# Three branch projections as Strassen pairs, summed by accumulating stores, in a hybrid decoder layer

## The chip, the cores and the metric

One core of one Trainium2 chip runs the whole program. The metric is the device time of one execution in microseconds (us). The kernel before took 1414.16, 1417.39 and 1422.7 us in three runs, median 1417.39.

## The reference

One layer of a decoder for 1024 prompt rows and 8 sample rows, all in float32. Three branches (gated linear attention "GLA", pooling, cross-attention) each give rows of width 1024; each is projected, multiplied by its own gate, and the three are added:

```python
proj = h @ w_in
...
branches = jnp.stack([br_gla, br_pool, br_x], axis=2)
bproj = jnp.einsum('btnw,nwd->btnd', branches, w_branch)
gates = jax.nn.sigmoid(merge.astype(jnp.float32)).reshape(B, T, N_BRANCH, D_MODEL)
merged = jnp.sum(gates * bproj.astype(jnp.float32), axis=2).astype(x.dtype)
y = merged @ w_out
return x + y, S.astype(x.dtype), new_hist
```

A last RMSNorm over x + y ends the program. The branch rows of GLA carry a per-channel gain (`gla_gain`).

## The kernel before, in words

**Numbers.** Every float32 operand of a large product is split into a high and a low part (`split`, L223 on ACT for the high part, L224 on DVE for the low one), and a product is three matmuls (`mm3`, L242 to L244): high by high, high by low, low by high.

**Pairs.** All the wide products up to the merge are done in pairs (`Pair`): a pair makes 256 output columns for all 1032 rows, by seven products of a Strassen-Winograd scheme. One product is 2 column halves by 4 steps by 3 matmuls, each 128 x 258. `seq` lists the products: (i, 1) to (i, 4), then (i+1, 0), then (i, 5) and (i, 6). `run_product` saves partial sums from PSUM with ACT (r1, r2, r3 at L686) and adds them up with DVE (L768, L787, L792, L797, L808 in the cases j = 1, 4, 5, 6). Product 1 to 4 end in the tile c1, which is finished in product 4; products 5 and 6 end in c2, finished in product 6. Products 0, 2 and 4 share the accumulator p.x, products 3 and 5 the accumulator p.z: product 5 adds to p.z, which the sums of product 4 have read together with r3.

Pairs 0 to 39 multiply by w_in and store their results to DRAM scratch: queries, keys, merge gates (`m_scr`), gated branch rows (`br_scr`). Pairs 40 to 43 project the cross-attention branch, pairs 44 to 47 the pooling branch (`ORDER` = 2, 1, 0). In `finish` the results are multiplied by sigmoid(merge), loaded by `factors` as tiles sg (L823) and passed through ACT (`sigmoids`); the product on DVE is L717, and the store to `acc_scr` is a DMA issued by POOL (L728), one for c1 and one for c2 of each pair. Between two branches `turnover` loads the next branch's rows and splits them as right-hand operands (tiles b and x by SP, v11, v21, v22 and four differences), spread over the products of the pairs around it.

**Units.** The third branch, GLA, is done in eight plain units of 128 output columns: eight steps over the inner dimension, three matmuls, chunks of 384, 384 and 264 rows. `branch_k` loads and splits the operand during the last pairs, with the gain applied in the split (L226, L227); `fetch` loads weights (wbr), gates (sig) and the two earlier sums (acc, acm) for a unit ahead; DVE adds and multiplies (L1598, L1606, L1607). The merged rows stay in SBUF and are split there (`mg_split`, tiles mg0h, mg0l and on), with a small copy on POOL of the sample columns (mgs).

**Output.** Sixteen blocks of 24 matmuls, 512 wide, multiply by w_out (column half hf 0, then hf 1), started for two row blocks in an inner range of 5 and then the rest (`begun`). The sample rows are two short blocks (8 and 9, L1662) that multiply by unsplit weights (wos, L1629). SP loads w_out (wor), the wos tiles, the final gain fg and the rows of x that are added (y, L1671). Each block is added to y by DVE (L1686) and squared by ACT (L1687); the norm follows and the stores.

**What sets the order.** PE and SP run in program order. ACT, DVE and POOL are ordered by a scheduler, held by `issue_after` edges. Buffers: pool E has 30 of 128 x 1032, ring R 15 of 128 x 516; PSUM accumulators PX six.

Of the kernel before, what the change touches and what calls it, by code (L numbers as in the profile page):

```python
# [40 lines left out]
O_Q, O_K, O_V, O_G, O_A, O_U, O_PG, O_XQ, O_XG, O_M = (  # L41
    0, 512, 1024, 2048, 3072, 3088, 4112, 5136, 6160, 7184)
EW = 1032
NBR = 2
EXP_LN_SET = 6


# [1 line left out]
def trunk_kernel(ctx: ExitStack, tc: tile.TileContext,  # L49
# [151 lines left out]
    PAIR = (P, 4, HT)  # L201
    xq_scr, v_scr = scratch(NH, "xqs", (NS, 256)), scratch(NH, "vs", (NS, 256))
    pt_scr = scratch(4 * NH, "pts", (8, 32, 4, 64))
    acc_scr = [scratch(4, f"acc{n}_", PAIR) for n in range(2)]
    mkv_scr = [scratch(NH, f"mkvs{o}", (P, 2, DV)) for o in range(2)]
    al_scr = scratch(2, "als", (P, HT))
    alp_scr = scratch(2, "alps", (P, 512))
# [124 lines left out]
        pairs += [Pair(cols_of(off + 2 * P * j), br_scr[n][j], gated=(n, j)) for j in range(4)]  # L332
    pairs.append(pairs.pop(27))
    for o, n in enumerate(ORDER[:NBR]):
        pairs += [Pair(w_branch[n][:, 2 * P * j:2 * P * (j + 1)], acc_scr[o][j], branch=(o, n, j)) for j in range(4)]
    NPAIR = len(pairs)
    TURNS = {39 + 4 * o: ORDER[o] for o in range(NBR)}

# [340 lines left out]
    def run_product(n):  # L679
# [18 lines left out]
        def finish(t, e):  # L698
            rows = (slice(0, 4, 3), slice(1, 3))[e]
            if p.s0 is not None:  # L700
                nc.gpsimd.tensor_copy(diagonal(smp[:, NS * p.s0:], e), t[:, :, 512:HT])
            if p.gated:
                n, g = p.gated
                for i in range(2):
                    ch, hf = divmod((0, 3, 1, 2)[2 * e + i], 2)
                    m = p.mix[e][i]
                    if n == 0:
                        x = m.rearrange("p (q w k) -> p w q k", q=4, w=4)
                        y = t[:, i, :512].rearrange("p (w q k) -> p w q k", q=4, w=4)
                        nc.vector.tensor_tensor(y, y, x, op=ALU.mult)  # L710
                    else:
                        nc.vector.tensor_tensor(t[:, i, :512], t[:, i, :512], m, op=ALU.mult)
                ss = diagonal(brs[n].rearrange("p k b -> p (k b)")[:, 2 * NS * g:], e)
                nc.vector.tensor_tensor(t[:, :, 512:HT], t[:, :, 512:HT], ss, op=ALU.mult)
            if p.branch:
                for i, sg in enumerate(p.mix[e]):
                    nc.vector.tensor_tensor(t[:, i], t[:, i], sg, op=ALU.mult)  # L717
            if p.turned:
                for i in range(2):
                    ch, hf = divmod((0, 3, 1, 2)[2 * e + i], 2)  # L720
                    r = R([512], name="vt")
                    nc.vector.transpose(r, t[:, i, :512])
                    for q in range(4):
                        c0 = ch * P + 32 * q
                        nc.gpsimd.dma_start(out=p.dst[512 * hf:512 * hf + 512, c0:c0 + 32].rearrange("(t r) c -> r t c", r=32),
                                            in_=r[32 * q:32 * q + 32].rearrange("r (t c) -> r t c", c=32))
                return
            nc.gpsimd.dma_start(out=p.dst[:, rows, :], in_=t)  # L728
# [791 lines left out]
    def branch_k(n, k):  # L1520
        hi, lo = E([2, HT], F32R, name=f"bh{n}"), E([2, HT], F32R, name=f"bl{n}")
        for hf in range(2):
            row = br_scr[n][k // 2][:, 2 * (k % 2) + hf]
            raw = loaded(row[:, :512], [512], "brr")
            split(hi[:, hf, :512], lo[:, hf, :512], raw, None if n else ggain[:, k:k + 1])
        nc.sync.dma_start(out=brs[n][:, k].rearrange("p (h b) -> p h b", h=2),
                          in_=br_scr[n][k // 2][:, 2 * (k % 2):2 * (k % 2) + 2, 512:HT])
        split(hi[:, :, 512:HT], lo[:, :, 512:HT], brs[n][:, k].rearrange("p (h b) -> p h b", h=2))
        return hi.rearrange("p h t -> p (h t)"), lo.rearrange("p h t -> p (h t)")

    units = [(o, ORDER[o], d) for o in range(NBR, 3) for d in range(NK)]
    inputs = {}

    def fetch(u):
        o, n, d = units[u]
        raw = RAW("wbr").rearrange("p a b -> p (a b)").rearrange("p (k n) -> p k n", k=NK)
        nc.sync.dma_start(out=raw, in_=w_branch[n][:, d * P:(d + 1) * P].rearrange("(k p) n -> p k n", p=P))
        w = []
        for i in range(2):
            h, l = W2("wbh"), W2("wbl")  # L1540
            split(h, l, raw[:, 4 * i:4 * i + 4])
            w.append((h, l))
        sig = E([TT], name="sig")
        nc.sync.dma_start(out=sig.rearrange("p (h t) -> p h t", h=2), in_=m_scr[n][d // 2][:, 2 * (d % 2):2 * (d % 2) + 2])
        acc = E([TT], name="acc")
        nc.sync.dma_start(out=acc.rearrange("p (h t) -> p h t", h=2),
                          in_=acc_scr[o - 1][d // 2][:, 2 * (d % 2):2 * (d % 2) + 2])
        more = [loaded(acc_scr[0][d // 2][:, 2 * (d % 2) + q], [HT], "acm") for q in range(2)] if NBR == 2 else []
        inputs[u] = w, sig, acc, more


    br = []
    for n in range(5, len(seq)):
        for _ in range({7: 2, 5: 1, 4: 1, 3: 1, 2: 1, 1: 1}.get(len(seq) - n, 0)):
            br.append(branch_k(ORDER[NBR], len(br)))
        if n == len(seq) - 2:
            fetch(0)
        emit(n)
        turnover(*seq[n])
    br.append(branch_k(ORDER[NBR], 7))  # L1560

    mg, late = [None] * NK, []
    mgs = R([NK, 32], name="mgs")
    for k in range(0, NK, 4):
        nc.gpsimd.memset(mgs[:, k:k + 4], 0.0)

    def mg_split(d, s):
        hi, lo = E([TT], F32R, name=f"mg{d}h"), E([TT], F32R, name=f"mg{d}l")
        split(hi, lo, s)
        mg[d] = hi, lo  # L1570
        nc.gpsimd.tensor_copy(mgs[:, d, :NS].rearrange("p (h b) -> p h b", h=2),
                              s.rearrange("p (h t) -> p h t", h=2)[:, :, 512:HT])

    wo = {}

    def w_out_unit(k, hf):
        raw = loaded(w_out[k * P:(k + 1) * P, 512 * hf:512 * hf + 512], [512], "wor", WS)
        if hf and k < 4:
            hi, lo = (W2("wo").rearrange("p a b -> p (a b)") for _ in range(2))
        elif hf:  # L1580
            e = E([2, 512], F32R, name="woe")
            hi, lo = e[:, 0], e[:, 1]
        elif k < 2:
            hi, lo = V([512], F32R, "woh"), V([512], F32R, "wol")
# [5 lines left out]
    for u, (o, n, d) in enumerate(units):  # L1590
        if d == 0 and o > NBR:
            br = [branch_k(n, k) for k in range(NK)]
        if u + 1 < len(units):
            fetch(u + 1)
        w, sig, acc, more = inputs.pop(u)
        act(sig, sig, AF.Sigmoid)
        for q, x in enumerate(more):
            nc.vector.tensor_tensor(acc[:, q * HT:(q + 1) * HT], acc[:, q * HT:(q + 1) * HT], x, op=ALU.add)  # L1598
        ts = [PX() for _ in CH]
        for k in range(NK):  # L1600
            lh, ll = (x[:, k % 4, :] for x in w[k // 4])
            for t, (c0, cw) in zip(ts, CH):
                mm3(t[:, :cw], lh, ll, br[k][0][:, c0:c0 + cw], br[k][1][:, c0:c0 + cw], k == 0, k == NK - 1)
        for t, (c0, cw) in zip(ts, CH):
            cs = slice(c0, c0 + cw)
            nc.vector.tensor_tensor(sig[:, cs], t[:, :cw], sig[:, cs], op=ALU.mult)  # L1606
            nc.vector.tensor_tensor(sig[:, cs], acc[:, cs], sig[:, cs], op=ALU.add)  # L1607
        if o < 2:
            nc.gpsimd.dma_start(out=acc_scr[o][d // 2][:, 2 * (d % 2):2 * (d % 2) + 2],
                                in_=sig.rearrange("p (h t) -> p h t", h=2))  # L1610
        else:
            if d < 5:
                mg_split(d, sig)
            else:
                late.append((d, sig))
            if d >= 2:
                w_out_unit(d - 2, 0)
    w_out_unit(6, 0)
    w_out_unit(7, 0)
    for d, s in late:  # L1620
        mg_split(d, s)
    own = []

    def own_weights(i):
# [5 lines left out]
            own.extend([w[:, 0], w[:, 1]])  # L1630

    own_weights(0)
    for k in range(NK):
        w_out_unit(k, 1)


    exp_ln_table()
# [9 lines left out]
            mm3(t[:, :b - a], th, tl, wh, wl, k == 0, k == NK - 1)  # L1647


    begun = [PX() for _ in range(2)]  # L1650
    for ks in (range(5), range(5, NK)):
        for tb in range(2):
            row_block(begun[tb], tb, 0, 0, 512, ks)
    for hf, order in enumerate(ORDERS):
        for tb in order:
            m = P if tb < 8 else NS
            if tb >= 8:
# [1 line left out]
                if tb == 8:  # L1659
                    ts = PX()  # L1660
                for j in range(4):
                    nc.tensor.matmul(ts[32 * j:32 * j + 32], lhsT=mgs[:, 4 * (tb - 8) + j], rhs=own.pop(0),  # L1662
                                     start=tb == 8, stop=tb == 9)
                if 2 * hf + tb < 11:
                    own_weights(2 * hf + tb - 7)
# [14 lines left out]
            for b in ends:  # L1680
                t = ts if tb == 8 else begun.pop(0) if begun else PX()
                cs = slice(512 * hf + a, 512 * hf + b)
                if tb < 8 and (hf or tb > 1):
# [58 lines left out]
```

## Time and profile before

| | |
|---|---|
| median of three runs | 1417.39 us (1414.16 to 1422.7) |
| profiled execution | 1417.57 us, span 1415.9 us, mean granted TensorE clock 0.992 |
| pairs 40 to 47 | 1064.46 to 1223.96 us |
| the eight units | 1223.96 to 1314.31 us |
| output, norm, last stores | 1314.31 to 1415.9 us |

The page gives for each engine its busy time, the span in 40 slices with the granted clock, the DMA queues, the chain of work that ended last, the costliest groups of instructions and the DMA issues with their median time to landing. A window view gives the busy time of each engine in a stretch. A row of the timeline is start, duration, engine, line, operation, output<-inputs, and in brackets the idle time before it and what ended it. DMA landing times are min, median and max over the transfers of a view. PE is the tensor engine's matmul side, PEld its weight loads, SPq and POOLq the queues of SyncE and GpSimd.

### The profile page before, as it was taken

Reading aid. Unit: us, or ns where it says so; the run is one execution under the profiler, and the core shown is the slowest. Engines: PE = TensorE matmul, PEld = TensorE weight load, DVE = VectorE, ACT = ScalarE, POOL = GpSimd, SP = SyncE. Lnnn points to the kernel's source line nnn. Section 1 sums busy time; section 2 is a strip of 40 time slices with the busy share of each in tenths; the row PEclk is TensorE's granted clock in tenths of the full one; section 3 lists DMA queues with packets and bytes.
Section 4 is the critical chain, followed back from the end, with each engine's and each line's share of the span. In section 5 each row is a group of like instructions: output and inputs, shape, how many; then the busy total and the mean of one; then the engine's idle time right before and its main releaser. Section 6 shows DMA issues by size and latency. Waiting matters only on the chain.

```text
span 1415.9 us, 29040 instructions
## 1 busy us (share of the span) xinstructions
PE 1390.2 (98%) x10817; PEld 1330.9 (94%) x10817; DVE 997.1 (70%) x2216; ACT 717.9 (51%) x1680; POOL 298.9 (21%) x529
## 2 busy tenths in 40 slices
PE   7999999999999999999999999999999999999998
PEld 6899898999899999999999999999999999999776
DVE  6966675758587777776766769786698896765336
ACT  6744444444466666655654544444456474632222
POOL 4254221335442232222231110101000000000000
PEclk9999999999999999999999999999999999999999
DMA  9367776967656455555555555468557785863633
GB/s 337 125 209 233 241 233 215 282 212 219 179 157 193 142 163 174 156 177 153 165 162 160 171 175 180 160 196 253 174 187 267 222 285 182 289 206 119 225 118 114
DMA packets 188377, 276.45 MB, mean 195 GB/s; under 512 B 20476, under 2 KB 132116, under 8 KB 188228
## 3 DMA queue, kind: packets, MB, share of 16 engines
q1 hardware_dynamic: 115420, 149.31, 33.9%
q0 software_dynamic: 26208, 78.94, 15.8%
q10 hardware_dynamic: 46608, 46.34, 11.4%
q8 instruction: 85, 1.39, 0.4%
q14 instruction: 56, 0.46, 0.1%
HBM read 192.18 MB, written 82.80 MB: 194 GB/s over the span
## 4 chain that ended last, share of the span: by engine, by line
PE 88%; DMA 6%; DVE 3%; issue 1%; ACT 1%; POOL 0%; SPq 0%; DVEq 0%; ACTq 0%
PE px L242 25%; PE px L243 25%; PE px L244 25%; PE pz L243 2%; PE pz L244 2%; PE pz L242 2%; DMA raw<-in_w_in_dram 2%; PE pz L1135 1%; PE pz L1114 1%; DMA wm<-in_w_mv_dram 1%; DMA qb<-xqs 1%; PE pz L962 1%; PE pz L1116 1%; DMA x<-brsc 1%; PE pz L467 0%
## 5 line engine op out<-in xcount | busy, mean ns | idle before, releaser
L686 ACT ACTIVATE r<-px 128x258 f32<-128x258 f32 x288 | 107.7, 377 | 62.4 <-PE px L244 58.1
L242 PE MATMUL px<-ot,s1h 128*128 128x258 f32 x320 | 94.0, 294 | 0.0
L303 DVE TENSOR_TENSOR ws<-raw 128x512 f32<-128x512 f32 x96 | 65.8, 686 | 39.1 <-DMA raw<-in_w_in_dram 27.7
L242 PE MATMUL px<-o,s4h 128*128 128x258 f32 x320 | 92.8, 290 | 0.0
L242 PE MATMUL px<-o,a11h 128*128 128x258 f32 x320 | 92.6, 289 | 0.0
L242 PE MATMUL px<-o,a12h 128*128 128x258 f32 x320 | 92.0, 288 | 0.4 <-DVE c L797 0.4
L242 PE MATMUL px<-ot,s3h 128*128 128x258 f32 x320 | 92.3, 288 | 0.0
L242 PE MATMUL px<-ot,s2h 128*128 128x258 f32 x320 | 92.3, 288 | 0.0
L242 PE MATMUL px<-ot,a22h 128*128 128x258 f32 x320 | 92.2, 288 | 0.0
L243 PE MATMUL px<-o,s4h 128*128 128x258 f32 x320 | 91.3, 285 | 0.0
L243 PE MATMUL px<-ot,s1h 128*128 128x258 f32 x320 | 91.0, 285 | 0.0
L244 PE MATMUL px<-ot,s3l 128*128 128x258 f32 x320 | 91.0, 284 | 0.0
L243 PE MATMUL px<-ot,s2h 128*128 128x258 f32 x320 | 90.4, 283 | 0.5 <-DVE ot L224 0.5
L244 PE MATMUL px<-ot,s1l 128*128 128x258 f32 x320 | 90.9, 284 | 0.0
L244 PE MATMUL px<-o,s4l 128*128 128x258 f32 x320 | 90.8, 284 | 0.0
L243 PE MATMUL px<-ot,a22h 128*128 128x258 f32 x320 | 90.8, 284 | 0.0
L243 PE MATMUL px<-ot,s3h 128*128 128x258 f32 x320 | 90.7, 284 | 0.0
L243 PE MATMUL px<-o,a11h 128*128 128x258 f32 x320 | 90.2, 282 | 0.3 <-DVE o L224 0.3
L244 PE MATMUL px<-o,a11l 128*128 128x258 f32 x320 | 90.4, 283 | 0.0
L244 PE MATMUL px<-ot,a22l 128*128 128x258 f32 x320 | 90.4, 283 | 0.0
L243 PE MATMUL px<-o,a12h 128*128 128x258 f32 x320 | 90.4, 282 | 0.0
L244 PE MATMUL px<-ot,s2l 128*128 128x258 f32 x320 | 90.3, 282 | 0.0
(538 smaller groups left out, 5228.8 us busy)
## 6 DMA issues: line engine op xcount, KB each, us to landing
raw<-in_w_in_dram ACTq DMA_DIRECT2D x72, 512.0 KB, 4.0
msc<-c POOLq DMA_DIRECT2D x24, 516.0 KB, 4.5
brsc<-c POOLq DMA_DIRECT2D x24, 516.0 KB, 4.3
b<-brsc SPq DMA_DIRECT2D x32, 258.0 KB, 5.0
sg<-msc SPq DMA_DIRECT2D x32, 258.0 KB, 6.9
acc<-c POOLq DMA_DIRECT2D x16, 516.0 KB, 6.9
kc<-in_cache_mem_k_dram SPq DMA_DIRECT2D x32, 256.0 KB, 5.1
vc<-in_cache_mem_v_dram SPq DMA_DIRECT2D x32, 256.0 KB, 5.2
```

The costliest lines, as they stand in the source:

```text
L242: nc.tensor.matmul(out, lhsT=lh, rhs=rh, start=start, stop=False, skip_group_check=more)
L243: nc.tensor.matmul(out, lhsT=lh, rhs=rl, start=False, stop=False, skip_group_check=more)
L244: nc.tensor.matmul(out, lhsT=ll, rhs=rh, start=False, stop=stop, skip_group_check=more)
L303: nc.vector.tensor_tensor(s, x, y, op=op)
L686: nc.scalar.activation(r, acc[c][:, :QT], AF.Copy)
L962: nc.tensor.matmul(t[32 * j:32 * j + 32, :DV], lhsT=pm[:, a, 4 * i + j, :], rhs=vc[j][:, a, :], start=a == 0, stop=a == 1)
L1114: nc.tensor.matmul(t[0:64, 0:P], lhsT=ki[:, 0:64], rhs=qi, start=True, stop=True)
L1116: nc.tensor.transpose(t[:, P:2 * P], kt, ident)
L1135: nc.tensor.matmul(to, lhsT=kiqi[:, 1, cs], rhs=st, start=False, stop=True)
```

## The change

All twelve branch pairs become Strassen pairs: pairs 40 to 51, with a third turnover to GLA's rows. The units, `branch_k` and `fetch` are gone. There is one scratch `acc_scr[j]` for each column group in place of one for each branch; the first branch stores into it plainly, the second and the third with `accum_op=ALU.add`, so that the DMA adds to what stands there (16 accumulating stores in all; in the new file L731, and L733 for the plain one). The GLA gain moves to one ACT operation of 128 x 512 ahead of the gating product of the GLA pairs, 16 in all. The merged rows are read back from the scratch: `merged_loaded` (SP, one load of 128 x 1032 for each of eight rows mg0 to mg7; two rows for each pair), `merged_split` (a copy of the sample columns on DVE, high part on ACT, low part on DVE). `closing` puts these and the w_out loads and splits of hf 0 between the products of pairs 49 to 51. Rows 6 and 7, of the last pair, are loaded after it. The output blocks begin with six row blocks over k 0 to 5, then k 6 and 7.

The diff, cut to what carries the change:

```diff
@@ tables and scratch
-NBR = 2
+NBR = 3
...
-    acc_scr = [scratch(4, f"acc{n}_", PAIR) for n in range(2)]
+    acc_scr = scratch(4, "acc", PAIR)
...
@@ finish
                     if n == 0:
+                        with tc.issue_after(last["hi"].ins):
+                            nc.scalar.activation(m, m, AF.Copy, scale=ggain[:, 2 * g + ch:2 * g + ch + 1])
...
-            nc.gpsimd.dma_start(out=p.dst[:, rows, :], in_=t)
+            if p.branch and p.branch[0]:
+                nc.gpsimd.dma_start(out=p.dst[:, rows, :], in_=t, accum_op=ALU.add)
+            else:
+                nc.gpsimd.dma_start(out=p.dst[:, rows, :], in_=t)
...
@@ in place of branch_k, fetch, the units and mg_split
+    def merged_loaded(d):
+        mgx[d] = E([2, HT], name=f"mg{d}l")
+        nc.sync.dma_start(out=mgx[d], in_=acc_scr[d // 2][:, 2 * (d % 2):2 * (d % 2) + 2])
+
+    def merged_split(d):
+        x, hi = mgx[d], E([2, HT], F32R, name=f"mg{d}h")
+        with tc.issue_after(last["hi"].ins), tc.issue_after(last["lo"].ins):
+            nc.vector.tensor_copy(mg["s"][:, d, :NS].rearrange("p (h b) -> p h b", h=2), x[:, :, 512:HT])
+            split(hi, x.bitcast(F32R), x)
+        mg[d] = tuple(y.rearrange("p h t -> p (h t)") for y in (hi, x.bitcast(F32R)))
...
+    def closing(i, j):
+        at = seq.index((i, j)) - seq.index((49, 0))
+        if at == 0:
+            mg["s"] = zeros()
+        if 1 <= at < 9:
+            w_out_split(at - 1, 0)
+        if 0 <= at < 8:
+            w_out_loaded(at, 0)
+        if (i, j) == (50, 6):
+            merged_loaded(0)
+            merged_loaded(1)
+        elif i == 51 and j in (2, 3):
+            merged_loaded(2 * j - 2)
+            merged_loaded(2 * j - 1)
+        if i == 51 and j in (2, 3, 4):
+            merged_split(2 * j - 4)
+            merged_split(2 * j - 3)
+
+    for n in range(5, len(seq)):
+        emit(n)
+        turnover(*seq[n])
+        closing(*seq[n])
+
+    for d in range(6, NK):
+        merged_loaded(d)
...
     own_weights(0)
+    for k in range(2):
+        w_out_loaded(k, 1)
     for k in range(NK):
-        w_out_unit(k, 1)
+        if k == 4:
+            for d in range(6, NK):
+                merged_split(d)
+        w_out_split(k, 1)
+        if k < 6:
+            w_out_loaded(k + 2, 1)
...
-    begun = [PX() for _ in range(2)]
-    for ks in (range(5), range(5, NK)):
-        for tb in range(2):
+    begun = [PX() for _ in range(6)]
+    for ks in (range(6), range(6, NK)):
+        for tb in range(6):
             row_block(begun[tb], tb, 0, 0, 512, ks)
```

How the instructions move, first on ACT in products 4 to 6 of the last pair. Before, in pair 47, the two r rows of L686 are the r3 saves of product 4 and of c = 0 and 1; between them stand splits of the next branch's operand (bh) and of unit weights (wbh); the rows of L808 are the end of product 6:

```order
L223 ACTIVATE bh_17162<-brs_114 128x2x4
L76 ACTIVATE sg<-sg 128x516 x2
L226 ACTIVATE bh_17210<-brr,vec 128x512 x2
L686 ACTIVATE r_17189<-px 128x258
L223 ACTIVATE bh_17210<-brs_114 128x2x4
L223 ACTIVATE wbh<-wbr 128x512
L686 ACTIVATE r_17204<-px 128x258
L223 ACTIVATE wbh<-wbr 128x512
L76 ACTIVATE sig<-sig 128x1032
L808 ACTIVATE c_17241<-px 128x258 x2
```

Now, in pair 51, the same two saves (r_18352, r_18367) and the same end (L813) stand among the splits of merged rows:

```order
L223 ACTIVATE mg2h<-mg2l 128x1032
L223 ACTIVATE mg3h<-mg3l 128x1032
L76 ACTIVATE sg<-sg 128x516 x2
L223 ACTIVATE mg4h<-mg4l 128x1032
L686 ACTIVATE r_18352<-px 128x258
L223 ACTIVATE mg5h<-mg5l 128x1032
L686 ACTIVATE r_18367<-px 128x258
L76 ACTIVATE sg<-sg 128x516 x2
L68 ACT_TABLE_LOAD
L813 ACTIVATE c_18381<-px 128x258 x2
```

So each r3 save has the split of a merged row ahead of it, mg4h and mg5h, which read what SP loads from the scratch. On DVE the low part of row 4 likewise stands ahead of the sums of L792.

The second place is SP's queue from the last units, or the last pair, to the output phase. Before, it loads gates and sums for the last unit (wbr, sig, acc, acm), then weights:

```order
L1537 DMA wbr<-in_w_branch_dram 128x8x128
L1544 DMA sig<-msc_3_197 128x1032
L1546 DMA acc<-acc_3_149 128x1032
L823 DMA acm<-acc_3_145 128x516 x2
L823 DMA wor<-in_w_out_dram 128x512 x4
L1629 DMA wos<-in_w_out_dram 128x2x512 x2
L823 DMA wor<-in_w_out_dram 128x512 x8
L1639 DMA fg<-in_final_gain_dram 128x1024
L1671 DMA y<-in_x_prompt_dram 128x1024 x2
L1629 DMA wos<-in_w_out_dram 128x2x512 x2
L1671 DMA y<-in_x_prompt_dram 128x1024 x3
```

Now the rows of the scratch stand in it:

```order
L1529 DMA mg3l<-acc_143 128x1032
L1529 DMA mg4l<-acc_144 128x1032
L1529 DMA mg5l<-acc_144 128x1032
L828 DMA sg<-msc_3_193 128x516 x2
L1529 DMA mg6l<-acc_145 128x1032
L1529 DMA mg7l<-acc_145 128x1032
L1590 DMA wos<-in_w_out_dram 128x2x512 x2
L828 DMA wor<-in_w_out_dram 128x512 x8
L1607 DMA fg<-in_final_gain_dram 128x1024
L1639 DMA y<-in_x_prompt_dram 128x1024 x2
L1590 DMA wos<-in_w_out_dram 128x2x512 x2
L1639 DMA y<-in_x_prompt_dram 128x1024 x3
```

The loads of mg4l and mg5l read the column group of pair 50, those of mg6l and mg7l that of pair 51, and wos, wor, fg and y stand behind the latter on the same queue.

More of the change, by code (lines that the diff above doesn't have):

```diff
@@ L334, in trunk_kernel @@
     for o, n in enumerate(ORDER[:NBR]):
-        pairs += [Pair(w_branch[n][:, 2 * P * j:2 * P * (j + 1)], acc_scr[o][j], branch=(o, n, j)) for j in range(4)]
+        pairs += [Pair(w_branch[n][:, 2 * P * j:2 * P * (j + 1)], acc_scr[j], branch=(o, n, j)) for j in range(4)]
     NPAIR = len(pairs)
@@ L1518, in trunk_kernel @@
         operand("t4", k, hA[k + 2])
[L1520 to L1549, printed above, removed]
@@ L1552, in trunk_kernel @@
[L1552 to L1572, printed above, removed]
@@ L1574, in trunk_kernel @@
-    wo = {}
-    def w_out_unit(k, hf):
-        raw = loaded(w_out[k * P:(k + 1) * P, 512 * hf:512 * hf + 512], [512], "wor", WS)
+    mg, mgx, wo = {}, {}, {}
+    def merged_loaded(d):
[7 more added lines that the diff above has]
+        mg[d] = tuple(y.rearrange("p h t -> p (h t)") for y in (hi, x.bitcast(F32R)))
@@ L1578, in w_out_unit, with w_out_loaded, w_out_split @@
+    def w_out_loaded(k, hf):
+        wo[k, hf] = loaded(w_out[k * P:(k + 1) * P, 512 * hf:512 * hf + 512], [512], "wor", WS if hf else None)
+    def w_out_split(k, hf):
         if hf and k < 4:
@@ L1582, in w_out_unit @@
             hi, lo = e[:, 0], e[:, 1]
-        elif k < 2:
-            hi, lo = V([512], F32R, "woh"), V([512], F32R, "wol")
-        else:
-            hi, lo = R([512], F32R, "woh"), R([512], F32R, "wol")
-        split(hi, lo, raw)
+        else:
+            hi, lo = ((V if k < 2 else R)([512], F32R, "wo") for _ in range(2))
+        with tc.issue_after(last["hi"].ins), tc.issue_after(last["lo"].ins):
+            split(hi, lo, wo[k, hf])
         wo[k, hf] = hi, lo
[L1590 to L1621, printed above, removed]
+    def zeros():
+        t = wk.tile([P, CT], F32, tag="st", name="mgs", bufs=2).rearrange("p (k b) -> p k b", k=NK)
+        nc.vector.memset(t, 0.0)
+        return t
+    def closing(i, j):
[15 more added lines that the diff above has]
+            merged_split(2 * j - 3)
@@ L1661, in trunk_kernel @@
                 for j in range(4):
-                    nc.tensor.matmul(ts[32 * j:32 * j + 32], lhsT=mgs[:, 4 * (tb - 8) + j], rhs=own.pop(0),
+                    nc.tensor.matmul(ts[32 * j:32 * j + 32], lhsT=mg["s"][:, 4 * (tb - 8) + j], rhs=own.pop(0),
                                      start=tb == 8, stop=tb == 9)
@@ L1682, in trunk_kernel @@
                 cs = slice(512 * hf + a, 512 * hf + b)
-                if tb < 8 and (hf or tb > 1):
+                if tb < 8 and (hf or tb > 5):
                     row_block(t, tb, hf, a, b, range(NK))
```

## The prediction

> **What bounds the kernel now.** I read the page first: its engine line, its clock row and the chain that ended last.
>
> ```profile
> PE 1390.2 (98%) x10817; PEld 1330.9 (94%) x10817; DVE 997.1 (70%) x2216; ACT 717.9 (51%) x1680; POOL 298.9 (21%) x529
> ...
> PEclk9999999999999999999999999999999999999999
> ...
> PE 88%; DMA 6%; DVE 3%; issue 1%; ACT 1%; POOL 0%; SPq 0%; DVEq 0%; ACTq 0%
> ```
>
> PE is busy 98% of the span and carries 88% of the chain, at full clock. So fewer PE microseconds shorten the kernel, unless PE then has to wait. The second view is the busy time by stretches: three Strassen pairs (42 to 44; each row begins with product 1 of a pair and ends before that of the next), the six products 1 to 6 of pair 47, the last one, the eight plain units, the output phase, and two short stretches early in the kernel.
>
> ```profile
> core 0: us, PE busy (x) PEld busy (x) DVE busy (x) ACT busy (x) POOL busy (x), PEclk, DMA share, GB/s
> 1104.83:1124.99 20.16, 20.16 (x171) 20.16 (x170) 17.73 (x32) 6.58 (x15) 1.28 (x2) 1.00 0.59 196
> 1124.99:1145.15 20.16, 20.16 (x170) 20.16 (x169) 19.80 (x32) 18.05 (x35) 1.28 (x2) 1.00 0.80 247
> 1145.15:1165.74 20.59, 20.44 (x170) 20.24 (x169) 20.16 (x36) 14.44 (x30) 1.28 (x2) 1.00 0.89 305
> 1206.13:1223.96 17.83, 17.60 (x147) 17.39 (x145) 15.65 (x31) 12.01 (x26) 1.65 (x4) 1.00 0.74 241
> 1223.96:1314.31 90.35, 90.35 (x578) 90.35 (x577) 52.90 (x93) 31.91 (x44) 3.85 (x8) 1.00 0.60 197
> 1314.31:1415.90 101.59, 94.84 (x442) 73.69 (x440) 46.90 (x107) 25.11 (x68) 0.53 (x1) 0.98 0.43 153
> 158.49:165.31 6.83, 5.56 (x26) 5.57 (x27) 5.58 (x13) 2.97 (x8) 2.10 (x4) 0.50 0.14 27
> 223.34:226.75 3.41, 3.41 (x17) 3.39 (x17) 2.29 (x7) 2.92 (x9) 0.00 (x0) 0.50 0.00 0
> ```
>
> A pair without a wait takes 20.16 us: seven products of 24 matmuls, so 2.88 us a product and 0.12 a matmul. The units run without a gap. The profiled execution took 1417.57 us, 0.18 above the median of the runs; sums below are made against it.
>
> **The arithmetic that goes.** The eight units' 90.35 us become four pairs: 4 x 20.16 = 80.64, so -9.7 us. The last pair's 17.83 us hold six products (17.28), so 0.55 us of waiting: ACT held PE up there with splits for the units, which go: -0.55. A turnover to the next branch's operands cost 20.59 - 20.16 = 0.43 (row 1145.15); the change adds one: +0.4, if its stores behave alike (below). In the output phase one wait goes too:
>
> ```profile
> 1342.41 0.39 PE L244 MATMUL px<-woh,mg6l 128*128 128x512 f32 x1
> 1343.10 0.40 PE L244 MATMUL px<-woh,mg7l 128*128 128x512 f32 x1
> 1343.42 1.85 PE L1662 MATMUL px<-wos,mgs 128*32 128x512 f32 x8
> ...
> 1373.19 1.06 PE L1662 MATMUL px<-wos,mgs 128*32 128x512 f32 x8
> ...
> DMA to landing us min/median/max: 6.2/8.2/10.2
> ```
>
> Three 512-wide matmuls take 0.69 us here (1342.41 to 1343.10), 0.23 each. The narrow ones of the sample rows' second half (row block 9, four instructions of two records each) take 1.85, and 1.06 in a later block: 0.8 us of waiting for their weight tile (the landing line is of the wos loads, the longest 10.2), which I take out and put back as a new wait below. Together -9.7 - 0.55 + 0.4 - 0.8 = -10.7, to 1406.9. The 16 scaling operations on ACT (the nearest row is a split of the same shape, 0.63 us) stand in stretches where ACT is half idle, and their operand is loaded early; I cost them at nothing, and bound them by 16 x 0.63 = 10 us of ACT, of which a tenth on the path would be 1 us. DVE gets the eight small copies from POOL and keeps its sums of about the same number: nothing.
>
> **What is added: stores that add.** No row of before shows such a transfer. The nearest rows are the plain stores of the same tiles by the same queue, here in the stretch of the branch pairs, and the loads that read as much:
>
> ```profile
> acc<-c POOLq DMA_DIRECT2D x16, 516.0 KB, 6.9
> sg<-msc SPq DMA_DIRECT2D x26, 258.0 KB, 7.0
> ...
> x<-brsc SPq DMA_DIRECT2D x6, 516.0 KB, 7.5
> ```
>
> ```profile
> DMA to landing us min/median/max: 2.9/6.9/8.9
> ```
>
> ```profile
> acc<-acc SPq DMA_DIRECT2D x1, 516.0 KB, 3.9
> ```
>
> The third row is one load of 516 KB with little beside it (3.9 us). So a store lands 2.9 to 8.9 us after its issue, median 6.9. One that adds has to fetch the old rows as well: the lower bound is the plain store (a gain I exclude, since it moves more), the upper a store and a load of the same bytes one after the other, 6.9 + 3.9 = 10.8, or 12 in traffic. Call the landing time of the second store of the last pair but one A, and that of the very last store A2. In the place of A, plain stores took 5.7:
>
> ```profile
> 1104.71 0.29 PE L244 MATMUL px<-vt4h,a22l 128*128 128x258 f32 x1
> ...
> 1107.18 0.56 POOL L728 DMA_DIRECT2D acc<-c  x1 [6.10 <-DVE c L717]
> ```
>
> ```profile
> DMA to landing us min/median/max: 5.7/5.7/5.7
> ```
>
> The store is issued 2.35 us after the pair's last product ends at 1104.83. I take A = 6.9, the group's median, and A2 = 4.1: the shortest plain one, since nothing else is then in flight, plus the same 1.2.
>
> The Trainium skill ("Collectives: The Full Stack", on why ReduceScatter is half of AllGather) says that an add inside a transfer costs because it reads two sources, and so halves the rate. It is measured there between cores, and no run here shows it for a store to the core's own memory. By it A would be about 11.4 and A2 5.8, which is the second rival.
>
> **The wait before product 5 of the last pair.** After pair 50's last product (time 0) come products 1 to 4 of pair 51, 4 x 2.88 = 11.52 us. Product 5 adds to the accumulator that the DVE sums at L792 must first have read; ahead of them ACT has the split of merged row 4 before the r3 save, and DVE its low part. Row 4 is loaded from the column that pair 50's second store writes. The lengths on that way:
>
> ```profile
> L223 ACT ACTIVATE v11h<-x 128x1032 fp32r<-128x1032 f32 x2 | 2.1, 1064 | 0.5 <-DMA acc<-c 0.5
> L224 DVE TENSOR_TENSOR x<-x,v21h 128x1032 fp32r<-128x1032 f32 x2 | 2.4, 1222 | 0.0
> L787 DVE TENSOR_TENSOR c<-px,r 128x258 f32<-128x258 f32 x14 | 5.9, 420 | 0.0
> L223 ACT ACTIVATE s4h<-ws 128x512 fp32r<-128x512 f32 x7 | 4.4, 629 | 2.9 <-PE px L244 1.2 <-PE px L243 0.9 <-ACT r L686 0.7
> ```
>
> Store issued at 2.35, landed at 2.35 + A, load 4.2 (a little over the 3.9), ACT split 1.06, DVE split 1.22, sum 0.42: 9.25 + A, against 11.52. The wait is A - 2.3: 4.6 us by A = 6.9, 0.6 by 2.9, 8.5 by 10.8. Behind the waiting ACT instruction stand both r3 saves, behind the DVE one both sums and the whole of the pair's end; PE has nothing else to do. Two earlier gaps of PE show what follows:
>
> ```profile
> 159.75 0.35 PE L953 MATMUL pz<-ident,ps 8*128 8x8 f32 x2 [3.15 <-DVE ps L942]
> ```
>
> ```profile
> 223.21 0.26 PE L953 MATMUL pz<-ident,ps 8*128 8x8 f32 x2 [2.34 <-DVE ps L942]
> ```
>
> After gaps of 3.15 and 2.34 us the rows 158.49 and 223.34 have a granted clock of 0.50, for 5.56 us of PE work after the gap in the one and 3.41 in the other; half of that is lost: 2.8 and 1.7. I add 1.7 to a wait of over 2 us, and keep 2.8 as the upper end. The Trainium skill ("TensorE: Matmul & The Clock Gate", Part 1) names about 3.4 us of idleness as what drops the clock; these gaps were shorter. By its figure the second wait would cost no clock (my sum would be 1.7 lower); the rows decide.
>
> **The wait in the output phase.** In before SP issues these in one row:
>
> ```profile
> 1312.90 0.90 SPq L1629 DMA_DIRECT2D wos<-in_w_out_dram  x2
> 1316.61 15.33 SPq L823 DMA_DIRECT2D wor<-in_w_out_dram  x8
> 1331.99 0.42 SPq L1639 DMA_DIRECT2D fg<-in_final_gain_dram  x1
> 1332.47 0.90 SPq L1671 DMA_DIRECT2D y<-in_x_prompt_dram  x2
> 1333.41 1.50 SPq L1629 DMA_DIRECT2D wos<-in_w_out_dram  x2
> ```
>
> The eight wor loads go two at a time through two buffers, so they pace the rest. From the first wos issue to the landing of the second of the later wos loads (issued at 1333.9, 10.2 long) pass 31.2 us. In the changed kernel the loads of merged rows 6 and 7 stand ahead of that row, and wait until the last pair's stores have landed. With the last product ending at time 0, I put the last store's issue at 1.3 (a sum of 0.42, a gating product of 0.69 and some hand-over), so it lands at 1.3 + A2; two issues of 0.7, then 31.2: the tile is there at 33.2 + A2, or 34 with the splits' later start. PE has six begun blocks, 108 + 36 matmuls at 0.232 = 33.4 us, then the narrow ones of block 8 (1.06) and half of those of block 9, which now follow at once: 34.9. The wait is about A2 - 1, so 3.1 us by A2 = 4.1, with 1.7 for the clock. The lower end is 0 (landing of 6.2 in place of 10.2), the upper A2 = 7: 6 + 2.8. Rows 6 and 7 themselves are split by about 20 + A2, before the 25 us that PE's first 108 matmuls cover, so they cost nothing unless A2 passes 5 to 6.
>
> **The third turnover.** Splitting the new right-hand operand waits for pair 46's first store to land (buffer c1); ahead of product 0 it has about 1.5 us of room at the second turnover's times (v11h above waited 0.5 us for such a store). With A within 1.5 us of a plain one it costs the 0.4 already counted; beyond that 1 to 3 us.
>
> **Sum.** 1417.57 - 10.7 + 4.6 + 1.7 + 3.1 + 1.7 = 1418.0, which stands for 1418 beside the median.
>
> **Rivals.** *Both waits nearly hidden:* the add costs nothing, A is near 2.9 and the wos loads land in 6.2. Then 1406.9 + 0.6 = 1407.5. For it: the last stores meet a nearly empty queue. Against: loads and sg fetches are in flight beside A, and the 5.7 of the quiet places is already 2.8 above it. *The adding store is much slower:* A = 11.4 and A2 = 5.8. The first wait is 9.1 + 2.8, the second 4.8 + 2.8, the turnover +1.5: 1406.9 + 21.0 = 1427.9. It turns slower than before by over 0.5% where A and A2 together exceed the taken 11 by about 6. For it: it must read and write 516 KB. Against: a read and a write of such rows at once need not be serial, and the DMA share in pairs 42 to 47 is 0.59 to 0.89, not full. *The ring:* twelve R buffers hold output weights from pair 49 on, and the sg loads of pairs 50 and 51 (7.0 from issue to landing, row above) come just in time; one late by 3 us adds 3 and its clock: 1418 + 3 to 6. *Only one of the two waits comes:* 1406.9 + 5 or 6, so 1412 to 1413, within 0.5% as the forecast is.
>
> **How the numbers follow.** A measurement of this kernel can tell about 0.5% (7 us) from no change: 1410.3 and 1424.5. Forecast with the one-wait case 0.38, hidden 0.27, slow stores 0.26, ring 0.09, of which a third is above 1424.5 and the rest within; with the slow stores that makes 0.29, and 0.44 lie within. The range takes in the hidden case at 1406.5 and the slow case with the larger A2 up to 1430.
>
> **What would show it.** Right: units gone, pairs 48 to 51 at 20.2 us each, PE gaps of 2 to 6 us ahead of (51,5) released by the L792 sum and ahead of the narrow matmuls released by a wos load, a clock of 0.5 behind each, and adding stores that land in 6 to 8 us. Wrong: no gap at (51,5), stores of over 10 us, or PE gaps inside pairs 46 to 50.

## The result and the profile after

The changed kernel takes 1428.61 us in the median of five runs (1424.86 to 1432.48), beside 1415.55 for the kernel before, now also from five runs; the ratio is 1.0093, with a 95% interval of 1.0072 to 1.0114. It is slower by 0.9%. The forecast was 1418, range 1406.5 to 1430, with no measurable change as the likeliest case: the range held, the likeliest case did not come. The profiled execution took 1432.48 us (span 1430.6), the slowest of the five.

PE's row on the page of the changed kernel:

```profile
PE 1387.8 (97%) x10913; PEld 1325.5 (93%) x10913; DVE 1017.8 (71%) x2243; ACT 744.5 (52%) x1746; POOL 304.6 (21%) x527
```

PE is busy 2.4 us less than before, and the span is 14.7 longer: what was added is waiting, and work at a lower clock, which counts as busy. The stretches say where. In the order of the rows: pairs 43 and 46, 47, 50, 51, then the output phase.

```profile
core 0: us, PE busy (x) PEld busy (x) DVE busy (x) ACT busy (x) POOL busy (x), PEclk, DMA share, GB/s
1126.49:1146.66 20.17, 20.17 (x171) 20.17 (x170) 19.81 (x32) 18.11 (x35) 1.28 (x2) 1.00 0.80 252
...
1187.69:1212.17 24.48, 21.96 (x170) 21.75 (x169) 18.55 (x34) 7.66 (x17) 2.08 (x2) 0.93 0.69 187
1212.17:1236.96 24.79, 21.98 (x171) 21.77 (x169) 19.42 (x32) 17.05 (x33) 2.08 (x2) 0.93 0.72 194
...
1277.38:1297.53 20.15, 20.15 (x170) 20.15 (x169) 13.36 (x23) 10.50 (x22) 2.09 (x2) 1.00 0.73 183
1297.53:1322.85 25.32, 19.03 (x147) 18.83 (x145) 14.76 (x25) 12.86 (x20) 2.09 (x2) 0.87 0.70 172
1322.85:1430.60 107.75, 96.93 (x442) 74.46 (x440) 45.80 (x104) 24.80 (x68) 0.89 (x1) 0.96 0.46 158
```

An undisturbed pair takes 20.16 us as before (20.15 in row 1277.38), six products 17.28. So pairs 46 and 47 lose 4.3 and 4.6 us, the last pair 8.0, and the output phase 7.0 against the 100.8 that it would take without the old wait. Each of the four rows has a clock below 1.00. Together that is 23.9 us. Add 0.9 us by which the branch pairs start later and 0.9 of small waits in pairs 41, 45 and 48, and take off the 11.1 us that did go (9.7 for the units, 0.55 and 0.8 for two old waits): that makes the 14.7 but for rounding.

PE's own rows at the four places (start, duration, operation, and in brackets the idle time before it and what ended it):

```profile
1204.78 0.39 PE L242 MATMUL px<-v22h,s4h 128*128 128x258 f32 x1 [2.52 <-DVE c L792]
...
1229.58 0.38 PE L242 MATMUL px<-v22h,s4h 128*128 128x258 f32 x1 [2.81 <-DVE c L792]
...
1315.51 0.58 PE L242 MATMUL px<-v22h,s4h 128*128 128x258 f32 x1 [6.29 <-DVE c L792]
...
1360.98 4.35 PE L1630 MATMUL px<-wos,mgs 128*32 128x512 f32 x16 [4.51 <-ACT px L1655]
```

The first three are product 5 of pairs 46, 47 and 51, which add to the accumulator that the sums of L792 must have read. In pair 46 those sums were late because DVE had stood at the pair's first sum, waiting for the buffer c1 of pair 45, and twelve differences of the turnover were queued behind it:

```profile
1183.73 1.19 POOL L731 DMA_DIRECT2D acc<-c  x1 [12.94 <-DVE c L719]
```

```profile
DMA to landing us min/median/max: 10.7/10.7/10.7
```

```profile
1194.55 0.43 DVE L773 TENSOR_TENSOR c<-px,r 128x258 f32<-128x258 f32 x1 [4.82 <-DMA acc<-c]
```

The adding store of c1, issued at 1183.73, landed 10.7 us later, and the DVE sum began 0.1 us after that. In pair 47 DVE waited 5.14 us for weights (raw) that were in flight together with two operand rows and an adding store:

```profile
1224.86 0.69 DVE L303 TENSOR_TENSOR ws<-raw 128x512 f32<-128x512 f32 x1 [5.14 <-DMA raw<-in_w_branch_dram]
```

In pair 51 it is the order that the prediction showed: ACT stood 5.49 us at the split of merged row 4, ahead of both r3 saves. Pair 50's second store had landed 9.0 us after its issue, and the load of the row came behind it.

```profile
1312.79 1.06 ACT L223 ACTIVATE mg4h<-mg4l 128x1032 fp32r<-128x1032 f32 x1 [5.49 <-DMA mg4l<-acc]
1313.76 0.37 ACT L686 ACTIVATE r<-px 128x258 f32<-128x258 f32 x1
```

In the output phase SP had the order forecast, each step later than in before:

```profile
1330.62 0.32 SPq L1529 DMA_DIRECT2D mg6l<-acc  x1
1331.03 0.38 SPq L1529 DMA_DIRECT2D mg7l<-acc  x1
1331.51 2.01 SPq L1590 DMA_DIRECT2D wos<-in_w_out_dram  x2
1333.57 17.24 SPq L828 DMA_DIRECT2D wor<-in_w_out_dram  x8
1350.86 0.42 SPq L1607 DMA_DIRECT2D fg<-in_final_gain_dram  x1
1351.34 0.90 SPq L1639 DMA_DIRECT2D y<-in_x_prompt_dram  x2
```

mg6l is issued when the last store has landed, 7.8 us after the last pair ends at 1322.85, and y at 1351.34. The narrow matmuls then waited for the first block's accumulator, whose sum on DVE waited for y:

```profile
1359.48 0.69 DVE L1654 TENSOR_TENSOR y<-px,y 128x512 f32<-128x512 f32 x1 [4.72 <-DMA y<-in_x_prompt_dram]
```

The wos tiles of the prediction came on top. The sixteen records take 4.35 us, where two groups of eight take 2 x 1.06: their weight loads waited 1.4 us for wos tiles (issued from 1352.28 on, landed after 9.7 and 10.6 us), and the granted clock from 1361 to 1366 was 0.50.

The adding stores themselves, 16 of them, and the plain ones of the first branch, eight:

```profile
DMA to landing us min/median/max: 6.0/8.4/10.7
```

```profile
DMA to landing us min/median/max: 5.1/6.9/9.1
```

### The profile page after: what moved, and what is told of

It reads as the page before. It is cut to its first block, busy times and chain, and to the rows that moved or that the text cites. A ratio compares the mean times of both kernels' runs of the same rounds, so it can differ in the third digit from the quotient of the medians.

```text
span 1430.6 us, 29300 instructions
## 1 busy us (share of the span) xinstructions
PE 1387.8 (97%) x10913; PEld 1325.5 (93%) x10913; DVE 1017.8 (71%) x2243; ACT 744.5 (52%) x1746; POOL 304.6 (21%) x527
## 4 chain that ended last, share of the span: by engine, by line
PE 31%; issue 17%; DMA 3%; DVE 2%; POOL 2%; ACT 1%; SPq 0%; POOLq 0%; DVEq 0%
PE px L242 9%; PE px L243 9%; PE px L244 9%; POOL acc L731 1%; DMA wor<-in_w_out_dram 1%; PE pz L242 1%; PE pz L244 1%; PE pz L243 1%; DVE b L623 1%; DMA y<-in_x_prompt_dram 1%; DMA raw<-in_w_branch_dram 1%; DMA raw<-in_w_in_dram 1%; DMA out_dram<-s 0%; PE px L1630 0%; DMA acc<-c 0%
## 5 line engine op out<-in xcount | busy, mean ns | idle before, releaser
L686 ACT ACTIVATE r<-px 128x258 f32<-128x258 f32 x312 | 115.9, 376 | 70.2 <-PE px L244 57.5
L303 DVE TENSOR_TENSOR ws<-raw 128x512 f32<-128x512 f32 x104 | 71.4, 686 | 44.6 <-DMA raw<-in_w_in_dram 26.1
L242 PE MATMUL px<-ot,s3h 128*128 128x258 f32 x320 | 92.1, 288 | 1.3 <-ACT r L686 1.3
L244 PE MATMUL px<-o,a12l 128*128 128x258 f32 x320 | 90.2, 282 | 0.0
```

The costliest lines, as they stand in the source:

```text
L242: nc.tensor.matmul(out, lhsT=lh, rhs=rh, start=start, stop=False, skip_group_check=more)
L244: nc.tensor.matmul(out, lhsT=ll, rhs=rh, start=False, stop=stop, skip_group_check=more)
L303: nc.vector.tensor_tensor(s, x, y, op=op)
L686: nc.scalar.activation(r, acc[c][:, :QT], AF.Copy)
```

## The experiments

Theory A: the adding store is what is slow, and it decides at buffers and loads that had little room. Theory B: the queues are in an order that waits, whatever the store costs. Ratios are against runs of the kernel before on the same chip.

**1. All stores plain.** It leaves out the sum of the branches.

```diff
-            if p.branch and p.branch[0]:
+            if p.branch and p.branch[0] > 2:
```

> All 24 stores of the branch pairs plain; leaves out the sum of the three branches (the scratch holds the last one only). In the changed kernel PE waited 2.5 us in pair 46, 2.8 in pair 47, 6.3 before product 5 of pair 51 and 4.5 before the sample rows, with the clock at half speed after each. Theory A (the adding store is what is slow): stores land in 5 to 8 us as in before, pairs 46 and 47 take 20.2 to 20.7 us in place of 24.5 and 24.8 (8 us less), the wait before product 5 falls by 2 to 3 us and the one in the output phase by as much; in all 11 to 14 us less, 1415 to 1418. Theory B (the order of the queues is what waits, the adding costs little): the four waits stay within 1 us each, 1425 to 1429.

Measured 1415.04 us, ratio 0.9997 (0.9976 to 1.0018): 13.6 us less than the changed kernel, as theory A has it. Pairs 46, 47 and 51 and the output phase:

```profile
1183.84:1204.03 20.19, 20.19 (x170) 20.19 (x169) 17.91 (x32) 6.84 (x15) 1.28 (x2) 1.00 0.59 190
1204.03:1227.94 23.91, 20.71 (x170) 20.30 (x169) 19.08 (x30) 17.47 (x35) 1.28 (x2) 1.00 0.67 212
...
1289.40:1311.18 21.78, 19.03 (x146) 18.82 (x145) 14.66 (x25) 12.86 (x20) 1.28 (x2) 0.92 0.56 195
1311.18:1415.00 103.82, 95.11 (x442) 73.80 (x440) 45.74 (x104) 24.83 (x68) 0.56 (x1) 0.98 0.45 163
```

Pair 46 is undisturbed, the last pair loses 4.5 us in place of 8.0, the output phase 3.0 in place of 7.0. Pair 47 missed: 23.91, with plain stores. And plain stores still leave the kernel no faster than before, so theory B holds for part of the rest: the order of the last pair and of SP costs 7.5 us (4.5 + 3.0) by itself. The landing times behind these two waits are those of pair 50's second store and of the very last:

```profile
DMA to landing us min/median/max: 5.4/5.4/5.4
```

```profile
DMA to landing us min/median/max: 3.0/3.0/3.0
```

**2. Only the third branch adds.** The first goes to a scratch of its own and is left out of the sum.

```diff
+    own_scr = scratch(4, "accx", PAIR)
...
-        pairs += [Pair(w_branch[n][:, 2 * P * j:2 * P * (j + 1)], acc_scr[j], branch=(o, n, j)) for j in range(4)]
+        pairs += [Pair(w_branch[n][:, 2 * P * j:2 * P * (j + 1)], acc_scr[j] if o else own_scr[j], branch=(o, n, j)) for j in range(4)]
...
-            if p.branch and p.branch[0]:
+            if p.branch and p.branch[0] > 1:
```

> The first branch goes to a scratch of its own and is left out of the sum, the second stores plainly, only the third adds (8 adding stores in place of 16). Theory A: the waits in pairs 46 and 47, which come from buffers held by pairs 44 to 46's adding stores, go (20.2 to 20.7 us each), 8 us less; the last pair and the output phase stay at 25.3 and 107.7: about 1420. Theory B: the third turnover has too much work for DVE whatever the stores do, pairs 46 and 47 stay above 23 us: 1427 or more.

Measured 1422.08, ratio 1.0057 (1.0038 to 1.0076): 0.36% or 5 us below the changed kernel by the two ratios, where 8 were expected. Pairs 46 and 47 are free, the last pair (26.07) and the output phase (106.85) stayed about as they were:

```profile
1185.47:1205.66 20.19, 20.19 (x171) 20.19 (x169) 18.27 (x33) 7.48 (x16) 1.28 (x2) 1.00 0.60 196
1205.66:1225.99 20.33, 20.33 (x171) 20.25 (x170) 18.71 (x30) 16.94 (x34) 1.28 (x2) 1.00 0.75 241
...
1287.48:1313.55 26.07, 19.70 (x147) 19.49 (x145) 14.75 (x25) 12.86 (x20) 2.08 (x2) 0.87 0.67 170
```

Theory A holds for the third turnover in pair 46 (20.19 in both runs with plain stores there). Pair 47 was 23.91 and 20.33 in the two, so plain stores do not always clear it.

**3. Splits of rows 4 and 5 behind the sums of product 4.**

```diff
...
-        if i == 51 and j in (2, 3, 4):
+        if i == 51 and j in (2, 3):
             merged_split(2 * j - 4)
             merged_split(2 * j - 3)
+        if (i, j) == (51, 5):
+            with tc.issue_after(last["sum"].ins):
+                merged_split(4)
+                merged_split(5)
```

> The splits of merged rows 4 and 5 come behind the r3 saves and the sums of product 4 of the last pair on both engines, otherwise the changed kernel. If the wait before product 5 is only this order, the last pair takes 17.3 to 18 us in place of 25.3 and the total falls by 7 to 8: about 1421. If the lateness of rows 4 and 5 only moves, PE waits for them at the first output block (they come about 3.5 us after product 5 was due and are needed 6.5 us after that), or the last stores and the loads behind them come no earlier: under 3 us less.

Measured 1420.31, ratio 1.0052 (1.0029 to 1.0075), with the adding stores as they were. By the two ratios that is 0.41% or 5.8 us below the changed kernel, a little less than the 7 to 8 expected; the nine runs spread from 1415.09 to 1426.63. The last pair and the output phase:

```profile
1289.28:1306.83 17.55, 17.54 (x146) 17.34 (x145) 13.59 (x25) 12.01 (x20) 2.09 (x2) 1.00 0.81 224
1306.83:1415.40 108.57, 97.67 (x442) 74.18 (x440) 46.81 (x105) 26.17 (x69) 0.89 (x1) 0.96 0.49 160
```

The wait of the last pair is gone whole, and 0.8 of its 7.8 us came back later. It was the order, made expensive by the store.

**4. wos and y ahead of merged rows 6 and 7 on SP.**

```diff
-    for d in range(6, NK):
-        merged_loaded(d)
...
     own_weights(0)
+    own_weights(1)
+    early = {}
+    for tb in range(2):
+        early[tb] = E([D], name="y")
+        nc.sync.dma_start(out=early[tb], in_=x_p[tb * P:(tb + 1) * P])
+    for d in range(6, NK):
+        merged_loaded(d)
...
```

> SP loads the four wos tiles and the first two y rows ahead of merged rows 6 and 7, which wait for the last store. If the late y and wos loads are what PE waits for at the sample rows, the output phase takes 101 to 102 us in place of 107.7 and the total falls by 5 to 6.5: about 1422.5. If the loads of rows 6 and 7 or the eight wor loads, two at a time, end as late as now and bind next, under 3 us less.

Measured 1419.69, ratio 1.0036 (1.0018 to 1.0054): 0.57% or 8 us below the changed kernel by the two ratios, more than expected. The output phase:

```profile
1322.74:1422.90 100.16, 93.83 (x442) 73.78 (x440) 45.55 (x104) 24.84 (x68) 0.89 (x1) 0.98 0.43 141
```

**5. The edits of runs 3 and 4 together.**

> The edits of the two runs before together (splits of rows 4 and 5 behind the sums of product 4; wos and y loads ahead of merged rows 6 and 7). If the two waits are independent the gains add: last pair 17.3 to 18 us, output phase 101 to 102, about 1413 to 1415, as fast as before. If the earlier end of the last pair brings the late loads forward against one another, the output phase keeps 2 us or more of waiting: 1416 or over. Pairs 46 and 47 stay at 24 to 28.

Measured 1416.21, ratio 1.0010 (0.9989 to 1.0031). The last pair took 17.55, the output phase 103.02: of the two waits' 15 us, 12.5 are gone. Now that the last pair ends earlier, PE waits 1.7 us in all for rows 6 and 7. That is the second of the two outcomes expected.

**6. The DVE order of the third turnover.** Runs 6 to 8 change run 5.

```diff
             elif step == (-2, 6):
                 block_loaded(n, "21", V)
-            elif step == (-1, 1):
+                if v == 3:
+                    difference(turn["12"], turn["11"], turn["11"], "t1")
+            elif step == (-1, 1) and v < 3:
...
             elif step == (0, 2):
                 operand_loaded(n, "21")
-            elif step == (0, 3):
+                if v == 3:
+                    operand_split(v, "t2")
+            elif step == (0, 3) and v < 3:
...
```

> The run above, and in the third turnover the four differences t1 one product earlier and the splits of t2 one product earlier, so that DVE does them while it waits for an adding store (pair 46) and for weights (pair 47). If the waits in pairs 46 and 47 come from DVE work piled up behind a waiting instruction, pairs 46 and 47 take 20.2 to 21.5 us in place of 24.5 and 24.8, 6 to 8 us less than the run above: about 1407, below before. If what is late there is the buffer or the transfer itself and not the pile, under 2 us less.

Measured 1410.60, ratio 0.9987 (0.9969 to 1.0005): 0.23% or 3 us below run 5 by the two ratios, with intervals that overlap. The stretches are clearer. Pairs 46, 47 and 48:

```profile
1183.84:1204.32 20.48, 20.44 (x170) 20.23 (x169) 17.07 (x31) 6.36 (x14) 2.08 (x2) 1.00 0.74 198
1204.32:1226.63 22.31, 20.37 (x170) 20.15 (x169) 19.37 (x31) 17.34 (x34) 2.08 (x2) 1.00 0.90 246
1226.63:1248.61 21.98, 21.98 (x169) 21.82 (x170) 21.32 (x38) 15.22 (x31) 2.09 (x2) 0.92 0.89 248
```

In pair 46 the store still lands late and DVE now has work to do meanwhile: 20.48 in place of 24.56 in run 5. Pair 47's wait became a shorter one at the start of pair 48 (PE 1.95 us for an ACT copy, the clock at 0.51 after it). The three pairs together gained 4.4 us on run 5, and the output phase lost 2.7 of it again (105.75 us; PE waited 2.22, 0.55 and 0.46 us for rows 6 and 7), so the gain fell short of the 6 to 8 us.

**7. Operand 21 loaded one product later.**

```diff
-            elif step == (0, 2):
+            elif step == (0, 2) and v < 3:
                 operand_loaded(n, "21")
             elif step == (0, 3):
+                if v == 3:
+                    operand_loaded(n, "21")
```

> The combined run without the DVE order change, but the two loads of operand 21 in the third turnover one product (2.9 us) later. If pair 47 waits because weights, operand rows and an adding store are in flight together, the weights (10.7 us before) land in 7 to 8 and pair 47 takes 21 to 22.5 in place of 24.8; pair 46 stays at 24.5. If the length of the adding store alone does it (buffer c2 held), pair 47 stays above 24.

Measured 1416.86, ratio 1.0024 (1.0004 to 1.0044). Pair 47:

```profile
1202.42:1231.42 29.00, 23.11 (x171) 22.91 (x169) 21.72 (x36) 18.35 (x35) 2.08 (x2) 0.88 0.70 184
```

It got worse by 4.2 us against the changed kernel, but runs 4 and 5, with the loads at their old place, had 27.94 and 23.44 there, and the total is not measurably different from run 5's. The run doesn't tell the two causes apart: the loads began 3.2 us into the pair, against 2.2 us before, since SP stood at an earlier load in both.

The profiles of the other runs say more. In every long pair 47 DVE waits for weights. Pair 43, at the same place of the second turnover, has the same wait in some profiles, although all its stores are plain. In run 9, and the landing time of those weights:

```profile
1136.88 0.69 DVE L303 TENSOR_TENSOR ws<-raw 128x512 f32<-128x512 f32 x1 [5.29 <-DMA raw<-in_w_branch_dram]
```

```profile
DMA to landing us min/median/max: 10.5/10.5/10.5
```

So a crowd of plain transfers can make the weights this late. With the DVE order of the changed kernel, pair 47 had the wait in all five profiles with adding stores there (4.82 to 6.74 us), and in the two with plain ones it was 4.55 and 1.62; in pair 43 it went from none to 5.29. How much of it the adding store makes stays open.

**8. Both edits of the turnover.**

> Both edits of the third turnover with the combined run. If either suffices for pair 47 it is as the run with the order change alone, about 1407; if each takes a part, 1 to 2 us below that; if the later operand loads now bind product 1 of pair 48 (product 1 uses operand 21), 1 to 3 us above it.

Measured 1412.25, ratio 0.9995 (0.9977 to 1.0013): no measurable difference from run 6. Pair 47 took 21.32 and pair 48 22.25, and DVE's wait for weights in pair 47 (2.26 us in run 6) was gone. It was gone in runs 10 and 12 too, which have this edit, and was 2.7 to 2.8 us in runs 9 and 11, which don't: here the later loads do help, by about 1.4 us over pairs 47 and 48 together (means of three profiles each).

**9 to 11. Rows 6 and 7 split ahead of the wor tiles** of run 6 (9), with operand 21 later as in run 8 (10), and run 9 with the DVE order in the second turnover too (11).

```diff
-        if k == 4:
+        if k == 0:
             for d in range(6, NK):
                 merged_split(d)
```

> The run with the combined edits and the DVE order of the third turnover, and the splits of merged rows 6 and 7 ahead of the eight wor splits on ACT and DVE. There the rows landed 6.2 us before their split began, and PE waited 2.2, 0.5 and 0.5 us for them with the clock low after: if the order alone makes that wait, the output phase takes 101 to 102 us in place of 105.7 and the total is 3.5 to 4.5 lower, 1406 to 1407, below before by 0.4 to 0.6%. If the last store, which landed after 10.2 us beside the early loads, still ends too late, or the wor splits now bind, under 1.5 us less.

> The same with operand 21 loaded one product later. The run with it but without the change of rows 6 and 7 had pair 47 1.0 us shorter and pair 48 0.3 longer than its neighbour: 1405.5 to 1407 if that holds, 1408 if it was chance.

> As the first run of this group, with the DVE order change in the second turnover too. Pairs 43 to 45 took 20.9 to 21.2 us where 20.2 is undisturbed: if the same pile of DVE work makes that, 2 us less than the first run (1404 to 1405). If what is late there are the plain stores and loads themselves, no difference within 1 us, or up to 2 us more where DVE now waits for the operand rows ahead of the end of a pair.

Measured 1413.79, 1414.46 and 1412.58, ratios 0.9978 (0.9957 to 0.9999), 0.9988 (0.9967 to 1.0009) and 0.9984 (0.9963 to 1.0005): none as fast as expected. The wait for rows 6 and 7 went in all three. Run 9's profile lost its time elsewhere (pair 43 took 26.09 us, the last pair 19.44); in runs 10 and 11 a next wait took its place, at the sample rows. PE's row there in run 10, and DVE's just ahead of it:

```profile
1341.77 3.64 PE L1647 MATMUL px<-wos,mgs 128*32 128x512 f32 x16 [5.00 <-ACT px L1675]
```

```profile
1337.79 0.69 DVE L224 TENSOR_TENSOR woe<-wor,woe 128x512 fp32r<-128x512 f32 x1 [2.54 <-ACT woe L223]
1339.66 0.69 DVE L224 TENSOR_TENSOR woe<-wor,woe 128x512 fp32r<-128x512 f32 x1 [1.17 <-ACT woe L223]
1340.27 1.28 DVE L1674 TENSOR_TENSOR y<-px,y 128x512 f32<-128x512 f32 x2
```

The y rows were there long before; their sums stood on DVE behind wor splits that wait for loads, two at a time. In run 11 pair 43 took 20.17 us, and 26.09 and 20.77 in runs 9 and 10; one profile of each doesn't settle what the DVE order does there.

**12. Run 10 with four wor tiles ahead of rows 6 and 7, and the second wos pair behind them.**

```diff
     own_weights(0)
-    own_weights(1)
...
+    for k in range(2):
+        w_out_loaded(k, 1)
+    for k in range(4):
+        w_out_split(k, 1)
+        if k < 2:
+            w_out_loaded(k + 2, 1)
     for d in range(6, NK):
         merged_loaded(d)
-    for k in range(2):
+    own_weights(1)
+    for k in range(4, 6):
         w_out_loaded(k, 1)
...
```

> As the run with rows 6 and 7 split first and operand 21 loaded later, but four of the eight wor tiles are loaded and split ahead of the loads of merged rows 6 and 7, and the second two wos tiles behind them. In that run rows 6 and 7 were in time and PE waited 5.0 us at the sample rows for the first y sum, which stood on DVE behind the last four wor splits. If those splits, paced by the two buffers, are what binds, they end about 8 us earlier, the wait goes, and the output phase takes 101 to 102 us in place of 107: about 1405 to 1408 in the profile, 0.5% below before by the median. If the last store is the limit in another way (rows 6 and 7 later than 25 us after the last pair), 2 us or more of waiting stays.

Measured 1409.39 in six runs, ratio 0.9949 (0.9934 to 0.9964): faster than the kernel before by 0.5% and than the changed one by 1.4% by the two ratios. Pairs 43, 46, 47 and 51 and the output phase:

```profile
1126.15:1151.33 25.18, 21.99 (x171) 21.47 (x170) 20.79 (x34) 18.36 (x35) 1.28 (x2) 0.93 0.68 208
...
1191.70:1211.89 20.19, 20.19 (x170) 20.19 (x169) 17.28 (x32) 6.47 (x15) 2.08 (x2) 1.00 0.73 193
1211.89:1232.32 20.43, 20.36 (x170) 20.15 (x169) 18.68 (x29) 17.09 (x34) 2.08 (x2) 1.00 0.94 247
...
1294.85:1312.41 17.56, 17.54 (x147) 17.34 (x145) 13.18 (x24) 11.37 (x18) 2.09 (x2) 1.00 0.89 249
1312.41:1412.40 99.99, 93.67 (x442) 73.72 (x440) 47.20 (x106) 26.92 (x71) 0.89 (x1) 0.99 0.51 170
```

The output phase has no wait left, though the last adding store still took 8.3 us. What this execution lost it lost in pair 43, 5 us, where all stores are plain.

## Why the prediction was right or wrong

**The arithmetic that goes.** Right. Pairs 48 to 50 of the third branch take 20.13 to 20.29 us where 20.16 was forecast, no time went to the scaling operations that shows, and run 12, a version of the change without waits in its last stages, is faster than before.

**The adding store.** One step that failed is "I take A = 6.9 ... and A2 = 4.1". A was 9.0 and A2 6.0: the add cost 3.6 us where a plain store took 5.4, and 3.0 where it took 3.0, not the 1.2 assumed in both. Both lie within the bounds; the value was taken from the nearest plain rows, and the row for what an add must do as well, a load of 3.9 us, was used only as the end of the range. The Trainium skill's rule ("Collectives: The Full Stack", on ReduceScatter) would have given A2 = 5.8 and A = 11.4: the quiet store agrees (6.0, twice the plain 3.0), the one in traffic is at 1.7 times its plain time.

**The wait before product 5.** Right in mechanism and in the formula. A - 2.3 gives 3.1 us for the plain 5.4 and 6.7 for 9.0; PE's idle time there was 2.75 and 6.29. The size was off by the store alone. The clock cost 1.7 more in both, as taken.

**The wait in the output phase.** The place and size of A2 - 1 were right (2.0 for the plain store and 5.0 for the adding one, against 2.11 and 4.51 measured), the tile named was not: y, one row ahead on the same queue, ended the wait, and the wos tiles only came on top. They landed up to 1363.4, so without y they alone would have held PE about as long; that the formula for wos met the wait for y so closely is in part luck. (Its 34.9 adds up to 35.0, which changes nothing.) The wait cost 7.0 us in all, where 4.8 had been taken.

**The third turnover.** This is the other step that failed: "it costs the 0.4 already counted; beyond that 1 to 3 us". Pairs 46 and 47 lost 8.9 us. The prediction looked at ACT's splits behind c1; in pair 46 it was DVE that stood at c1, with twelve differences queued behind. It takes both to make the 4.3 us there: with plain stores the loss is gone (20.19, runs 1 and 2), and with the adding store nearly as late (10.1 us) but the pile moved it is all but gone as well (20.48, run 6). Pair 47 waits for weights in a crowd of transfers. That the adding store makes the crowd too slow is not shown: run 1 had the loss there with plain stores, and pair 43 has it in some profiles. Two signs that the prediction had named for being wrong came here, gaps of PE inside pairs 46 and 47 and stores of over 10 us (10.7).

**The rivals.** The second one, the adding store much slower, was priced at 1427.9 and came within 1 us of the median with other shares: its first wait 9.1 + 2.8 was 8.0, its second 4.8 + 2.8 was 7.0, and its turnover of 1.5 was 8.9. That the total came so near is luck: the first wait was priced 3.9 us too high and the turnover 7.4 too low. One argument against it was misread: the DMA share of pairs 42 to 47 went from 0.47 (pair 46) to 0.89, not from 0.59. The ring did not come: pairs 48 to 50 took 20.1 to 20.3.

## What to carry to other kernels

Compared place by place with run 1, after pair 50 and at the end, an adding store held its source buffer 1.7 and 2 times as long as a plain one; the medians over pairs 44 to 51 are 8.4 and 5.9 us, 1.4 times. So before using it, list each buffer with its room and everything that is queued behind the instruction that waits for it, on every engine. A load that must wait for the last store belongs behind the loads that could go at once and are needed as early (run 12 put it in the middle of the w_out tiles), and a split that waits for a load belongs behind whatever releases PE. And when one wait is removed look for the next in line: here it took five changes of order until 7 of the 10 us of saved PE work showed.

## What the runs showed of the hardware

The clock fell after shorter idle times of PE than the two rows of before: in run 6 a gap of 1.95 us was followed by a stretch at 0.51,

```profile
1227.50:1231.00 3.50, 3.50 (x19) 3.50 (x19) 3.50 (x7) 3.01 (x6) 0.00 (x0) 0.51 1.09 250
```

while one of 2.11 us in run 1, ended at 1346.88, was not:

```profile
1346.90:1353.00 6.10, 5.78 (x28) 2.63 (x29) 1.86 (x3) 1.78 (x5) 0.00 (x0) 1.00 1.03 400
```

The Trainium skill ("TensorE: Matmul & The Clock Gate", Part 1) names about 3.4 us of idleness; the drop in run 6 came after a shorter gap. What sets one gap apart from the other is not shown.

The same code ahead of the branch pairs took between 1057.0 and 1065.4 us in the profiles of these kernels, and pair 43, with plain stores in all of them, between 20.16 and 26.09. That is why a change of 10 us in one stage needs the stretch of that stage, and not one total, to be seen.
